# Two small tiles take 64 bytes each, and the output projections' activations start elsewhere in SBUF

## The chip, the cores and the metric

The kernel runs on one core of one Trainium2 chip, as one launch. Its time is device microseconds of one execution; given is the median of a few runs. A separate execution is recorded by the hardware profiler, and all rows below come from that one.

## The reference, cut to what matters

The program is a two-layer decoder trunk over 256 tokens and 1024 channels. Layer 0 mixes tokens by multi-scale retention, layer 1 by a gated delta rule (DeltaNet). A dense SwiGLU channel mixer of 2816 hidden channels follows each. Every sub-layer ends in one large output projection:

```python
    return y.astype(hdn.dtype) @ w_out                      # retention: (256 x 2048) @ (2048 x 1024)
    return o.astype(hdn.dtype) @ w_out                      # DeltaNet:  (256 x 2048) @ (2048 x 1024)
    return (jax.nn.silu(gate) * up) @ w_out                 # SwiGLU:    (256 x 2816) @ (2816 x 1024)
for i in range(DEPTH):                                      # DEPTH = 2
    h = h + mix
    h = h + swiglu(rmsnorm(h, norm_ffn[i]), ffn_w_in[i], ffn_w_out[i])
return rmsnorm(h, norm_final)
```

Everything is float32.

## The kernel before

**Split products.** Each float32 operand of a projection is split into two parts of TensorE's float32r type, hi (rounded) and lo (what is left). A product is then three matmuls (`mm3`, lines 139 to 141): hi by hi, lo by hi, hi by lo. The weights' parts are `whi` and `wlo`, made by ScalarE (line 131) and VectorE (line 133) from a slab `raw` of 512 KB that a DMA brings in. The activations' parts are `xh`/`xl` for the input projections, `yh`/`yl` for the output projection of retention and of DeltaNet, `hh`/`hl` for that of SwiGLU.

**Who is stationary.** In `proj_tok` a block of 128 tokens by 128 channels of the activations is the stationary operand (it is loaded into the array; the trace calls this LDWEIGHTS on PEld), and 512 columns of the weights stream past. So the row `mm<-whi,hh` is a matmul with `whi` moving and `hh` stationary. In `proj_chan` it is the other way round, with 256 columns moving. The four output projections are all made by `out_proj` with `proj_tok`. One slab holds two blocks of 128 channels, and serves 2 blocks x 3 products x 2 halves of the tokens, 12 matmuls. A SwiGLU output projection has 22 channel blocks x 3 x 2 token halves x 2 column halves = 264 matmuls, that of retention or DeltaNet 16 x 3 x 2 x 2 = 192.

**Who waits for whom.** Three buffers each of `raw`, `whi` and `wlo` rotate. TensorE runs its instructions in the order of the program. In the output projections it works through the slabs; transposes and small matmuls of the mixer's last pieces stand between them in the DeltaNet one.

**Where tiles lie.** A tile pool hands out bytes of each partition one tile after another, and each tile's size is rounded up to 32 bytes. The pools of the constants, the weights (`wp`), the input activations (`xp`) and the small scalars (`sm`) live as long as the kernel. Behind them, one pool for each sub-layer (`self.ph`) is opened and closed again. So the end of `sm` is the start of every sub-layer's pool. `rstd` (line 308) allots the tile `ms` (128 x 2 floats) from `sm`, in two buffers; `head` in `retention` allots `brs` (128 x 1 float) from the sub-layer's pool, in two buffers, ahead of `yh` and `yl`.

Of the kernel before, what the change touches and what calls it, by code (L numbers as in the profile page):

```python
# [10 lines left out]
F32 = mybir.dt.float32  # L11
# [6 lines left out]
P = 128  # L18
D = 1024
S = 256  # L20
NT = S // P
# [40 lines left out]
class Trunk:  # L62
# [245 lines left out]
    def rstd(self):  # L308

        nc = self.nc  # L310
        m = self.sm.tile([P, NT], F32, name="ms", tag="ms")
        nc.vector.scalar_tensor_tensor(m, self.ss[:, 0], EPS, self.ss[:, 1], ALU.add, ALU.add)
        r = self.sm.tile([P, NT], F32, name="r", tag="r")
        nc.gpsimd.tensor_tensor(r, m, self.mhalf[:, 0:NT], ALU.pow)
        self.r = r
# [190 lines left out]
    def retention(self, nxt):  # L506
# [4 lines left out]
        tile_ = lambda shape, name, **k: self.ph.tile(shape, F32, name=name, **k)  # L511
# [40 lines left out]
        def head(h, k, q):  # L552
            for _ in range(3):
                yield
            sp = self.psip()
            for j, (c0, i0) in enumerate(((0, 0), (S, P))):
                for d in range(2):
                    nc.tensor.matmul(sp[:, c0:c0 + S - i0], k[:, d, j * P:(j + 1) * P], q[:, d, i0:S],
                                     start=d == 0, stop=d == 1)
            sT = tile_([P, 384], "sT", bufs=2)  # L560
            nc.vector.tensor_tensor(sT[:, 0:S], sp[:, 0:S], b["dec"][:, h], ALU.mult)
            nc.vector.tensor_tensor(sT[:, S:S + P], sp[:, S:S + P], b["dec"][:, h, 0:P], ALU.mult)
            yield
            for t in range(NT):
                op = self.psip()
                nc.tensor.matmul(op, sT[:, t * P:(t + 1) * P], b["v"][0][:, h], start=True, stop=t == 0)
                if t == 1:
                    nc.tensor.matmul(op, sT[:, S:S + P], b["v"][1][:, h], start=False, stop=True)
                st, mv = tile_([P, 6], "bst", bufs=2), tile_([P, 2], "bmv", bufs=2)
                nc.vector.bn_stats(st, op)  # L570
                nc.vector.bn_aggr(mv, st)
                nc.vector.tensor_scalar(mv[:, 1:2], mv[:, 1:2], EPS, None, ALU.add)
                rs = tile_([P, 1], "brs", bufs=2)
                nc.gpsimd.tensor_tensor(rs, mv[:, 1:2], self.mhalf[:, 0:1], ALU.pow)
                yield
                nc.vector.tensor_scalar(b["o"][t][:, h], op, mv[:, 0:1], rs, ALU.subtract, ALU.mult)

        for h in range(4):
            kq = []

            def k_done(ps, kq=kq):
                kq.append(rotate(ps))

            def q_done(ps, kq=kq, h=h):
                self.spawn(head(h, kq[0], rotate(ps)))

            self.proj_chan(w_in, 1024 + h * 256, self.xT, k_done)
            self.proj_chan(w_in, h * 256, self.xT, q_done)
# [633 lines left out]
```

## Time and profile before

| | |
|---|---|
| median of 3 runs | 865.16 us (862.71 to 866.62) |
| the profiled execution, its own time | 866.91 us |
| span of the profile, first to last instruction | 865.2 us |
| TensorE busy | 835.5 us (97%), 4805 matmuls |
| VectorE, ScalarE busy | 567.5 us (66%), 448.8 us (52%) |
| mean granted clock | 0.994 |

The times of the stages, from the span's start: the output projection of retention runs from about 164 to 213 us, that of the first SwiGLU from 337 to 401 us, that of DeltaNet from 624 to 675 us, that of the second SwiGLU from 796 to 858 us. A matmul's row gives its start and a modelled length; matmuls overlap in the array, so the next one starts well before the length is over, and the pace is read from start to start. In a table of windows an instruction counts in a stretch if any of it lies there.

### The profile page before, as it was taken

How to read it: one execution, taken by the hardware profiler on the slowest of the kernel's cores; microseconds unless marked ns; L12 is line 12 of the kernel's file. 1: busy time of each engine (PE TensorE's matmuls, PEld its weight loads, DVE VectorE, ACT ScalarE, POOL GpSimd, SP SyncE). 2: the span in 40 equal slices, each digit the busy share in tenths (PEclk: the TensorE clock that was granted, in tenths of full speed). 3: DMA queues.
4: the chain of work that ended last, by engine and by line, in shares of the span. 5: the costliest groups of instructions: out<-in, count | busy, mean ns of one | idle time of the engine just before them, and what ended most of it. 6: DMA issues, size and time to landing. Idle time of an engine off the chain costs nothing.

```text
span 865.2 us, 12647 instructions
## 1 busy us (share of the span) xinstructions
PE 835.5 (97%) x4805; PEld 709.1 (82%) x4805; DVE 567.5 (66%) x834; ACT 448.8 (52%) x760; POOL 56.9 (7%) x56
## 2 busy tenths in 40 slices
PE   8999999899999999999999989999899999999996
PEld 7789987788788778786999878998788888889885
DVE  4777876575566555555789899864656655666553
ACT  5553234465444443444587755488854644444443
POOL 0000000000000000000117241000110000000000
PEclk9999999999999999999999999999999999999999
DMA  7676456976687778765455734742045687788762
GB/s 257 196 205 172 126 147 171 234 243 179 198 241 230 213 236 230 229 195 148 124 150 140 201 110 117 212 132 90 1 135 182 194 240 228 227 238 245 232 194 74
DMA packets 182367, 158.21 MB, mean 183 GB/s; under 512 B 72690, under 2 KB 126499, under 8 KB 182307
## 3 DMA queue, kind: packets, MB, share of 16 engines
q1 hardware_dynamic: 182130, 157.34, 61.8%
q8 instruction: 37, 0.61, 0.3%
q14 instruction: 24, 0.19, 0.1%
q10 hardware_dynamic: 144, 0.07, 0.0%
q0 software_dynamic: 32, 0.01, 0.0%
HBM read 147.96 MB, written 9.44 MB: 182 GB/s over the span
## 4 chain that ended last, share of the span: by engine, by line
PE 69%; DVE 13%; DMA 8%; ACT 4%; issue 3%; SPq 2%; POOL 1%; POOLq 0%; ACTq 0%; DVEq 0%
PE mm L141 21%; PE mm L140 21%; PE mm L139 21%; DVE wlo L133 5%; DMA ht<-zd 2%; DVE cacc L751 2%; DVE pr L840 2%; SPq L215 2%; ACT whi L131 1%; DMA zd<-z 1%; PE tp L200 1%; DMA raw<-gdn_w_in 1%; DMA raw<-ffn_w_in 1%; DVE Vb L842 1%; PE ip L979 1%
## 5 line engine op out<-in xcount | busy, mean ns | idle before, releaser
L133 DVE TENSOR_TENSOR wlo<-raw,whi 128x1024 fp32r<-128x1024 f32 x260 | 318.0, 1229 | 197.6 <-ACT whi L131 188.6
L131 ACT CAST whi<-raw 128x1024 fp32r<-128x1024 f32 x260 | 271.6, 1050 | 290.8 <-PE mm L140 148.7
L139 PE MATMUL mm<-whi,xh 128*128 128x512 f32 (+1 forms) x576 | 219.1, 383 | 5.0 <-ACT whi L131 4.1
L140 PE MATMUL mm<-whi,xl 128*128 128x512 f32 (+1 forms) x576 | 219.2, 381 | 0.5 <-DVE xl L337 0.3
L141 PE MATMUL mm<-wlo,xh 128*128 128x512 f32 (+1 forms) x576 | 203.4, 381 | 1.8 <-DVE wlo L133 1.7
L139 PEld LDWEIGHTS mm<-whi,xh 128*128 128x128 f32 x576 | 108.9, 189 | 27.1 <-ACT whi L131 6.8
L141 PEld LDWEIGHTS mm<-wlo,xh 128*128 128x128 f32 x576 | 108.6, 189 | 24.9 <-DVE wlo L133 5.1
L140 PEld LDWEIGHTS mm<-whi,xl 128*128 128x128 f32 x576 | 109.0, 189 | 21.6 <-issue 0.7
L139 PE MATMUL mm<-xh,whi 128*128 128x256 f32 x384 | 111.7, 291 | 0.0
L140 PE MATMUL mm<-xh,wlo 128*128 128x256 f32 x384 | 110.1, 287 | 0.3 <-DVE wlo L133 0.2
L141 PE MATMUL mm<-xl,whi 128*128 128x256 f32 x384 | 109.8, 286 | 0.0
L140 PEld LDWEIGHTS mm<-xh,wlo 128*128 128x128 f32 x384 | 74.0, 193 | 2.3 <-issue 1.0
L139 PEld LDWEIGHTS mm<-xh,whi 128*128 128x128 f32 x384 | 74.1, 193 | 1.3 <-issue 0.5
L141 PEld LDWEIGHTS mm<-xl,whi 128*128 128x128 f32 x384 | 74.1, 193 | 0.3
L139 PE MATMUL mm<-whi,hh 128*128 128x512 f32 x176 | 69.6, 396 | 1.0 <-ACT whi L131 1.0
L140 PE MATMUL mm<-whi,hl 128*128 128x512 f32 x176 | 69.5, 395 | 0.0
L141 PE MATMUL mm<-wlo,hh 128*128 128x512 f32 x176 | 63.6, 396 | 0.3 <-DVE wlo L133 0.3
L139 PE MATMUL mm<-whi,yh 128*128 128x512 f32 x128 | 50.0, 398 | 1.0 <-ACT yh L336 1.0
L751 DVE SCALAR_TENSOR_TENSOR cacc<-mm,conv,cacc 128x253 f32<-128x253 f32 (+2 forms) x96 | 45.6, 509 | 8.1 <-ACT cacc L748 7.5
L140 PE MATMUL mm<-whi,yl 128*128 128x512 f32 x128 | 50.6, 395 | 0.0
L141 PE MATMUL mm<-wlo,yh 128*128 128x512 f32 x128 | 48.7, 397 | 0.0
L139 PEld LDWEIGHTS mm<-whi,hh 128*128 128x128 f32 x176 | 33.0, 188 | 9.3 <-ACT whi L131 1.4
(238 smaller groups left out, 857.9 us busy)
## 6 DMA issues: line engine op xcount, KB each, us to landing
raw<-ffn_w_in SPq DMA_DIRECT2D x88, 512.0 KB, 4.4
raw<-ret_w_in SPq DMA_DIRECT2D x48, 512.0 KB, 4.4
raw<-gdn_w_in SPq DMA_DIRECT2D x48, 512.0 KB, 4.0
raw<-ffn_w_out SPq DMA_DIRECT2D x44, 512.0 KB, 4.3
raw<-ret_w_out SPq DMA_DIRECT2D x16, 512.0 KB, 4.3
raw<-gdn_w_out SPq DMA_DIRECT2D x16, 512.0 KB, 3.6
zd<-z SPq DMA_DIRECT2D x52, 128.0 KB, 3.7
ht<-zd SPq DMA_DIRECT2D x13, 512.0 KB, 5.4
```

What stands on the lines that cost most here:

```text
L131: nc.scalar.copy(hi, raw)
L133: lo_ = nc.vector.tensor_tensor(lo, raw, hi.bitcast(F32), ALU.subtract)
L139: t.matmul(out, lh, rh, start=first, stop=False)
L140: t.matmul(out, ll, rh, start=False, stop=False)
L141: self.last_mm = t.matmul(out, lh, rl, start=False, stop=last).ins
L200: self.nc.tensor.transpose(out, in_, self.ident[:n, :n])
L215: nc.sync.dma_start(to[q], z[32 * q:32 * q + 32, 0:nk].rearrange("p k t g i -> p (k t) g i"))
L751: self.nc.vector.scalar_tensor_tensor(acc[:, s:S], ps[:, 0:S - s], cw[:, i, blk:blk + 1], acc[:, s:S], ALU.mult, ALU.add)
L840: V.tensor_tensor(tmp, Vb[:, 0:n, i:i + 1].broadcast_to([P, n, m]), Ab[:, n:32, i].unsqueeze(1).broadcast_to([P, n, m]), ALU.mult)
L842: V.tensor_tensor(Vb[:, 0:n, n:32], Vb[:, 0:n, n:32], tmp, ALU.subtract)
L979: T.matmul(f4(op[:, 2 * j:2 * j + 2]), x(2 * hg + j), f4(st[:, 2 * j:2 * j + 2]), start=True, stop=True)
```

## The change

The tile `ms` is allotted with 16 floats a partition and its first two are used, and the tile `brs` is allotted with 16 floats and its first is used. Two buffers of `ms` so take 128 bytes and not 64, and two of `brs` likewise. Nothing else is edited. On every engine the same instructions stand in the same order with the same waits, so no rows of the order are shown.

```diff
     def rstd(self):
 
         nc = self.nc
-        m = self.sm.tile([P, NT], F32, name="ms", tag="ms")
+
+
+        m = self.sm.tile([P, 16], F32, name="ms", tag="ms")[:, 0:NT]
         nc.vector.scalar_tensor_tensor(m, self.ss[:, 0], EPS, self.ss[:, 1], ALU.add, ALU.add)
...
-                rs = tile_([P, 1], "brs", bufs=2)
+                rs = tile_([P, 16], "brs", bufs=2)[:, 0:1]
                 nc.gpsimd.tensor_tensor(rs, mv[:, 1:2], self.mhalf[:, 0:1], ALU.pow)
```

What moves are start bytes in a partition, read from the two built programs. All tiles of the sub-layers' pools move up by 64, in retention's pool those behind `brs` by 128. Steps between the 128 x 128 blocks of an operand are multiples of 512 bytes, so each block has its tile's remainder.

| tile | start before | mod 128 | mod 256 | start after | mod 128 | mod 256 |
|---|---|---|---|---|---|---|
| `whi`, `wlo` (first buffers) | 44096, 56384 | 64 | 64 | the same | 64 | 64 |
| `xh`, `xl` | 68672, 76864 | 64 | 64 | the same | 64 | 64 |
| `yh`, `yl` of retention | 157248, 173632 | 64 | 64 | 157376, 173760 | 64 | 192 |
| `hh`, `hl`, both SwiGLU layers | 87424, 109952 | 0 | 128 | 87488, 110016 | 64 | 192 |
| `yh` of DeltaNet (first of four) | 157056 | 0 | 128 | 157120 | 64 | 192 |
| `wh`, stationary in DeltaNet's gates, blocks of 128 bytes | 29760 | 64 | 64 and 192 in turn | the same | 64 | 64 and 192 in turn |
| `D`, `A`, `v`, `Vf`, `kT`, `qT`, `Vb` of DeltaNet; `silu`, `z`, `ht` of SwiGLU | | 0 | | | 64 | |
| `cacc`, `vc`, `uu`, `du`, `S1`, `qs`, `pr` of DeltaNet | | 64 | | | 0 | |
| `silu`, `z`, `ht` of retention's end | | 64 | | | 64 | |

## Rows read from the trace of the kernel before

**Rows 1.** The page: busy time by engine; chain that ended last, by engine.
```profile
PE 835.5 (97%) x4805; PEld 709.1 (82%) x4805; DVE 567.5 (66%) x834; ACT 448.8 (52%) x760; POOL 56.9 (7%) x56
...
PE 69%; DVE 13%; DMA 8%; ACT 4%; issue 3%; SPq 2%; POOL 1%; POOLq 0%; ACTq 0%; DVEq 0%
```

**Rows 2.** Groups by line and shape, TensorE: busy us, mean ns | idle before.
```profile
L139 PE MATMUL mm<-whi,xh 128*128 128x512 f32 x512 | 201.0, 396 | 5.0 <-ACT whi L131 4.1 <-ACT xh L655 0.7
...
L139 PE MATMUL mm<-whi,hh 128*128 128x512 f32 x176 | 69.6, 396 | 1.0 <-ACT whi L131 1.0
...
L139 PE MATMUL mm<-whi,yh 128*128 128x512 f32 x128 | 50.0, 398 | 1.0 <-ACT yh L336 1.0
```

**Rows 3.** Windows: length, PE, PEld, DVE, ACT, POOL, granted clock, DMA share, GB/s.
```profile
725.00:775.00 50.00, 50.00 (x222) 41.13 (x221) 28.84 (x26) 23.40 (x25) 0.00 (x0) 1.00 0.81 229
800.00:850.00 50.00, 50.00 (x216) 40.12 (x215) 26.46 (x27) 22.09 (x25) 0.00 (x0) 1.00 0.61 198
350.00:400.00 50.00, 50.00 (x215) 40.03 (x214) 25.88 (x28) 21.73 (x28) 0.00 (x0) 1.00 0.65 206
```

**Rows 4.** Timeline, TensorE, retention's output projection: start us, length us, what.
```profile
174.46 0.40 PE L139 MATMUL mm<-whi,yh 128*128 128x512 f32 x1
...
175.41 0.39 PE L139 MATMUL mm<-whi,yh 128*128 128x512 f32 x1
...
177.02 0.39 PE L140 MATMUL mm<-whi,yl 128*128 128x512 f32 x1
...
179.51 0.39 PE L140 MATMUL mm<-whi,yl 128*128 128x512 f32 x1
```

**Rows 5.** Timeline, TensorE, DeltaNet's output projection.
```profile
667.00 0.39 PE L139 MATMUL mm<-whi,yh 128*128 128x512 f32 x1
...
669.57 0.39 PE L141 MATMUL mm<-wlo,yh 128*128 128x512 f32 x1
```

**Rows 6.** Timeline, TensorE, first SwiGLU's output projection; in brackets idle time before.
```profile
346.97 0.50 PE L139 MATMUL mm<-whi,hh 128*128 128x512 f32 x1 [0.96 <-ACT whi L131]
...
348.42 0.50 PE L141 MATMUL mm<-wlo,hh 128*128 128x512 f32 x1 [0.26 <-DVE wlo L133]
```

**Rows 7.** Chain that ended last, first SwiGLU's output projection: start us, us, what.
```profile
335.59 3.23 DMA zd<-z
338.90 6.01 DMA ht<-zd
...
398.17 0.25 PE mm L141
```

**Rows 8.** Chain that ended last, end of DeltaNet's output projection.
```profile
670.43 0.25 PE mm L141
670.70 0.70 DVE h L360
```

**Rows 9.** Timeline, TensorE, DeltaNet's gates: 32 stationary columns.
```profile
414.90 0.28 PE L139 MATMUL ip<-xh,wh 128*32 128x256 f32 x1
...
415.81 0.28 PE L141 MATMUL ip<-xl,wh 128*32 128x256 f32 x1
```

**Rows 10.** Groups by line and shape, ScalarE.
```profile
L131 ACT CAST whi<-raw 128x1024 fp32r<-128x1024 f32 x260 | 271.6, 1050 | 290.8 <-PE mm L140 148.7 <-PE mm L141 39.1 <-DMA raw<-ffn_w_in 36.8
...
L440 ACT ACTIVATE silu<-mm,r 128x512 f32<-128x512 f32 x20 | 13.7, 685 | 10.3 <-PE mm L141 10.3
...
L617 ACT ACTIVATE silu<-mm,r 128x512 f32<-128x512 f32 x8 | 5.5, 684 | 2.4 <-PE mm L141 2.4
...
L932 ACT COPY D<-tp 128x512 f32<-128x512 f32 x8 | 4.8, 599 | 0.8 <-PE tp L200 0.8
...
L990 ACT COPY S<-ip 128x512 f32<-128x512 f32 x4 | 2.3, 570 | 0.4 <-PE ip L979 0.4
```

**Rows 11.** Groups by line and shape, VectorE.
```profile
L133 DVE TENSOR_TENSOR wlo<-raw,whi 128x1024 fp32r<-128x1024 f32 x260 | 318.0, 1229 | 197.6 <-ACT whi L131 188.6
...
L751 DVE SCALAR_TENSOR_TENSOR cacc<-mm,conv,cacc 128x254 f32<-128x254 f32 x32 | 14.9, 476 | 0.4
```

## The prediction

> **What bounds the kernel now.** I read the page's busy times and its chain first, to know which engine a saving has to be on. TensorE is busy for 835.5 of 865.2 us, and 69% of the chain is its own [rows 1]. Since the change leaves every instruction and every wait where it was, the question is only whether some instruction runs at another pace from another address. So the second view is the groups by shape, TensorE alone. There the stationary operand's name makes no difference to see: 396 ns with `xh`, 396 with `hh`, 398 with `yh` [rows 2]. But these lengths are modelled and overlap (0.39 us long, a start each 0.23 us), so the pace must be counted, not read. Third, therefore, equal windows of 50 us that hold nothing but matmuls of 512 columns: 222 matmuls touch a stretch of the second SwiGLU's input projection (`xh`, `xl` stationary), only 216 and 215 touch stretches of the two SwiGLU output projections (`hh`, `hl` stationary) [rows 3]. TensorE is busy for all of each, at granted clock 1.00, which is the 2.4 GHz level. About 0.39/0.23 = 1.7 matmuls are in flight at any time, so a stretch is touched by that many more than start in it: 50,000/(222 - 1.7) = 227.0 ns, 50,000/(216 - 1.7) = 233.3 ns, and 50,000/(215 - 1.7) = 234.4 ns in the first SwiGLU. I take 233.3 for both and 6.3 ns as the difference, 2.7% of a matmul.
>
> Is it the address, or is it the stage? The two output projections with `yh` tell, since the same code makes them and one lies at 64 modulo 128, the other at 0. In retention (64) two starts that are eleven matmuls apart lie at 177.02 and 179.51: 2.49/11 = 226 ns [rows 4]. In DeltaNet (0) eleven matmuls take from 667.00 to 669.57: 2.57/11 = 234 ns [rows 5]. So the longer pace goes with a stationary operand at 0 in three stages of three, the shorter one with 64 in both. An output projection as such does not have the longer pace. The clock is the same, and the input projection, with the shorter pace, moves more by DMA than the outputs (229 against 198 and 206 GB/s [rows 3]), so DMA traffic isn't the reason either.
>
> **The change part by part.** The padding itself costs nothing: no instruction is added, and the sub-layers' pools still fit. What it moves are start bytes.
>
> *Second SwiGLU's output projection.* 264 matmuls, all on the chain to the end, no wait among them: 264 x 6.3 = 1.66 us.
>
> *First SwiGLU's.* The chain comes into this stage over the last block of hidden channels (a store of `z` at 335.59, the load of `ht` until 344.91) [rows 7], and TensorE stands twice, until 346.97 for `whi` and until 348.42 for `wlo` [rows 6]. What is saved ahead of that is given back in those waits. From there to 398.17, where the chain leaves TensorE [rows 7], I count (398.17 - 348.42)/0.2333 = 213 starts, one of them late: 210 x 6.3 = 1.32 us.
>
> *DeltaNet's.* 192 matmuls. The chain leaves TensorE with the one at 670.43 [rows 8], 15 before the stage's last, so 177 x 6.3 = 1.12 us.
>
> *Restarts.* Retention's stage shows that the shorter pace isn't there at once: from 174.46 to 175.41, shortly after transposes, four matmuls take 238 ns each, and by 177.02 it is 226 [rows 4]. I take six matmuls at the longer pace, 6 ns each, after each break. DeltaNet's stage is broken up by transposes and small matmuls seven times, the SwiGLU ones three times in all: 10 x 6 x 6 ns = 0.36 us that aren't saved. Sum: 1.66 + 1.32 + 1.12 - 0.36 = 3.74 us.
>
> *Retention's output projection.* `yh` and `yl` move by 128 and stay at 64 modulo 128. I take zero; the bounds are 0 and +192 x 6.3 = +1.2 us (second rival).
>
> *VectorE, ScalarE and the DMAs on moved tiles.* The nearest rows for ScalarE are the same activation with `silu` at 0 in SwiGLU (685 ns) and at 64 in retention (684) [rows 10]: no effect. Of PSUM copies the one to `D` (at 0) takes 599 and the one to `S1` (at 64) 570 [rows 10]; since some tiles go from 0 to 64 and as many from 64 to 0, I take zero, with bounds of 29 ns either way. On the 96 taps like the 476 ns row [rows 11], whose `cacc` goes from 64 to 0, and some 70 other instructions of this kind, that is at most 166 x 29 ns = 4.8 us of work either way, mostly beside TensorE. VectorE and ScalarE hold 17% of the whole chain [rows 1], so I keep 4.8 x 0.17 = 0.8 us either way on the path.
>
> *What is late next.* If TensorE needs a slab of 12 matmuls in 12 x 227 = 2.72 us and not 2.80, the cast (1.05 us [rows 10]) and the difference (1.23 us [rows 11]) per slab still fit. The DMA engines are at 0.61 to 0.65 there and run at 0.81 elsewhere without holding TensorE up [rows 3]. So the gain stays, but for DeltaNet's, where TensorE could catch up with the mixer's last pieces; I have no row that gives their slack and leave up to 0.5 us of the 1.12 in doubt.
>
> The profiled execution of 866.91 us (span 865.2, 1.7 around it) would go to 863.2. It lies 1.75 above the median of the runs shown; on that median, 865.16 - 3.74 = 861.4 us, or 0.43% less.
>
> **Rivals.**
>
> *The address isn't the cause: no change, 865.2 us.* For it: the lengths of rows 2 are equal, and the link to the address rests on five stages. Against it: both paces appear in the same code [rows 4, 5]. In the Trainium skill, the page "TensorE: Matmul & The Clock Gate", section "Part 2: What happens when you issue a matmul", gives TensorE two independent SBUF read ports, so that loading the next weights takes nothing from the running matmul, and a gap of 512/2.4 plus about 2.5 ns, some 216 ns, in which no address occurs. By that rule this rival would be the forecast. The trace doesn't agree: it has 227 and 233 ns [rows 3]. The page "SBUF — State Buffer", section "Door 1: The DMA port swizzle", has lines of 16 bytes; 0 and 64 both start a line, so by it too nothing would change.
>
> *It is another modulus: slower.* All operands with the short pace lie at 64 modulo 256, with `whi` and `wlo`, and all with the long one at 128. Afterwards `hh`, `hl` and every `yh`, `yl` lie at 192, which no big matmul of this trace has. If the stationary block must share the weights' place modulo 256, the three stages stay as they are and retention's joins them: 192 x 6.3 = +1.2 us, 866.4 us. It decides the sign as long as the mixer's bound helps by less than 1.2 us; to pass 0.5% (4.3 us) it would need 192 to be worse than 128 by another 912 matmuls' 3.4 ns each. Against it: in DeltaNet's gates the blocks of `wh` lie at 64 and 192 modulo 256 in turn, and eight matmuls over three blocks take 0.91 us, 114 ns each, without a step between blocks [rows 9]. These have 32 stationary columns and not 128, so they weigh little. For 128: 512 moving columns of 4 bytes pass in at most 227 ns, so 64 bytes of them in at most 7.1, and the step between the two paces is 6.3, about one such piece.
>
> *Gained, and given back in DeltaNet's mixer.* The gain of 3.74 is halved by slower taps (+0.8), and by waits for the mixer's last pieces (0.5) and for slabs (0.5): 3.74 - 1.8 = 1.9 us, 863.3 us.
>
> **How the numbers follow.** The forecast has 0.68, no change 0.15, another modulus 0.09, gained and half given back 0.08. The runs shown spread over 3.9 us, so a measured median may be 1 us off; about 0.5% is what a measurement of this kernel can tell from no change, here 4.3 us, a time under 860.8. The forecast's own range, with 0.8 either way for the mixer and 1 for the measurement, is 859.4 to 863.2. To hold eight in ten I go up to 865.7, which takes in more than half of the no-change case, and down to 859.0. Faster by over 0.5%: the forecast lies 0.6 us short of it, about 0.45 of its 0.68 chance, with a little from the rest: 0.33. Slower by over 0.5%: 0.04, nearly all from another modulus. Within: 0.63.
>
> **What would show it.** Right: a 50 us window inside either SwiGLU output projection is touched by 222 matmuls and not 216; eleven matmuls in DeltaNet's output projection take 2.49 us; retention's still do; the waits of the first SwiGLU output projection grow by 0.3 us; everything between 401 and 624 us is as long as before. Wrong: windows still with 216 (no change), or retention's pace at 233 (another modulus), or the right windows with a longer stretch from 401 to 624 us (given back).

## The result, and the profile after

The changed kernel takes 871.29 us (median of 5 runs, 870.13 to 871.83), the kernel before takes 864.72 us (862.35 to 866.62) beside it: ratio 1.0084, 95% interval 1.0062 to 1.0107. It is slower by 6.6 us; 861.4 us was forecast. Its profiled execution took 871.12 us, with a span of 869.4 us, 4.2 more than before. In the profile's page no engine is busy for over 1 us more than before [rows 1], but in the chain that ended last the share of TensorE falls from 69% to 53%, and that of the DMAs rises from 8% to 15%:

```profile
PE 836.4 (96%) x4805; PEld 707.4 (81%) x4805; DVE 567.7 (65%) x834; ACT 448.7 (52%) x760; POOL 57.0 (7%) x56
...
PE 53%; DVE 16%; DMA 15%; ACT 6%; SPq 5%; issue 4%; POOL 1%; POOLq 0%; ACTq 0%; DVEq 0%
```

The windows answer the forecast's first question. These are the input projection of the second SwiGLU and the output projection of the first, with the columns of [rows 3], and then two stretches of DeltaNet's mixer that are spoken of below:

```profile
725.00:775.00 50.00, 50.00 (x222) 41.33 (x221) 30.03 (x28) 23.41 (x25) 0.00 (x0) 1.00 0.82 230
350.00:400.00 50.00, 50.00 (x216) 40.23 (x215) 26.00 (x28) 21.74 (x28) 0.00 (x0) 1.00 0.61 207
...
559.00:562.00 3.00, 3.00 (x71) 2.96 (x64) 2.91 (x8) 1.52 (x2) 0.00 (x0) 0.67 0.71 226
562.00:565.00 3.00, 3.00 (x54) 2.87 (x55) 2.94 (x5) 2.18 (x4) 0.00 (x0) 0.76 0.00 0
```

The output projection is touched by 216 matmuls, as before (215), and not by 222: nothing was gained. Retention's, which had the shorter pace [rows 4], has lost it. In TensorE's timeline of the changed kernel, first retention's output projection, then DeltaNet's, then the place in DeltaNet's mixer:

```profile
177.62 0.39 PE L139 MATMUL mm<-whi,yh 128*128 128x512 f32 x1
...
180.41 0.39 PE L139 MATMUL mm<-whi,yh 128*128 128x512 f32 x1
...
666.34 0.40 PE L139 MATMUL mm<-whi,yh 128*128 128x512 f32 x1
...
669.14 0.40 PE L139 MATMUL mm<-whi,yh 128*128 128x512 f32 x1
...
556.34 0.28 PE L140 MATMUL mm<-xh,wlo 128*128 128x256 f32 x1
558.76 1.20 PE L878 MATMUL ip<-Vc,A 32*32 32x32 f32 x64 [2.14 <-DMA Vc<-Vd]
...
560.40 0.41 PE L140 MATMUL mm<-xh,wlo 128*128 128x256 f32 x1
560.62 0.41 PE L141 MATMUL mm<-xl,whi 128*128 128x256 f32 x1
```

Between the first two rows, and between the next two, lie twelve starts each: 2.79/12 = 232.5 ns in retention (227 before), 2.80/12 = 233.3 ns in DeltaNet (as before). Over all steps of a stage between two big matmuls the means are 232.7, 233.2, 232.6 and 233.2 ns in the four output projections; before they were 227.2, 233.3, 233.3 and 233.3.

The last rows show something that the forecast had no term for. TensorE stands 2.14 us for `Vc`, the solved triangular blocks of DeltaNet, which come back from HBM in another layout. After that the granted clock is 0.67 and 0.76 in the two windows above, so for a part of these 6 us it was at its 1.2 GHz level, and matmuls of 256 columns start each 0.21 to 0.22 us. In the timeline of before the same place has a wait of 0.56 us and a start each 0.12 us:

```profile
557.15 1.20 PE L876 MATMUL ip<-Vc,A 32*32 32x32 f32 x64 [0.56 <-DMA Vc<-Vd]
...
558.62 0.28 PE L140 MATMUL mm<-xh,wlo 128*128 128x256 f32 x1
558.74 0.28 PE L141 MATMUL mm<-xl,whi 128*128 128x256 f32 x1
```

A fall of the clock is nothing that only the changed kernel has, though. Three windows, first of before, then after:

```profile
162.00:167.00 5.00, 4.57 (x13) 3.62 (x14) 4.47 (x7) 4.22 (x8) 0.00 (x0) 0.66 0.87 215
527.00:532.00 5.00, 4.02 (x22) 4.02 (x23) 4.90 (x8) 4.12 (x10) 1.83 (x1) 0.66 0.26 72
557.00:565.00 8.00, 7.26 (x190) 7.01 (x191) 7.81 (x14) 4.95 (x8) 0.00 (x0) 1.00 0.45 128
```

```profile
162.00:167.00 5.00, 4.89 (x21) 3.66 (x22) 4.78 (x7) 4.64 (x8) 0.00 (x0) 1.00 0.73 148
527.00:532.00 5.00, 3.77 (x30) 3.57 (x31) 4.90 (x8) 4.50 (x12) 1.84 (x1) 1.00 0.28 68
557.00:565.00 8.00, 6.24 (x126) 6.10 (x128) 6.20 (x12) 3.70 (x6) 0.00 (x0) 0.79 0.57 138
```

The profile of before has two such falls elsewhere, ahead of retention's output projection and in DeltaNet's mixer, and the profile after has one at `Vc` in place of them. So the clock at `Vc` makes this stretch longer, but in these two profiles it is no part of what the whole kernel lost.

Why `Vc` is late, the chain that ended last says. Before, then after (start, us, what):

```profile
547.85 4.82 DMA Vd<-Vb
552.69 4.33 DMA Vc<-Vd
```

```profile
547.86 5.34 DMA Vd<-Vb
553.22 5.40 DMA Vc<-Vd
```

The pair starts at the same time as before and ends 1.6 us later. `Vc` is written to SBUF in pieces of 128 bytes; so are the stores `zd<-z` of the transposes read from it. The trace records every DMA packet. Those of 128 bytes have a mean duration, before and after, of 12.34 and 13.30 ns in the first SwiGLU's input projection, 12.48 and 13.26 in the second's, 12.12 and 13.33 ns in the store of DeltaNet's `A` (4096 packets at 479 us), and 12.91 and 15.86 ns in the load of `Vc`. These are just the ones whose SBUF side went from 0 to 64 modulo 128. Retention's `z` was at 64 and stayed there: 13.3 and 13.2 ns.

A mean hides how it comes about. With `Vc` at 0 all 4096 packets of its load take 11 to 13 ns; after the change 73% of them still do, and 18% take over 20 ns (27.6 in the mean). And one load doesn't fit: the 1,024 packets of `wr`, the raw weights of DeltaNet's gates, are written in pieces of 128 bytes to a start at 64 modulo 128 (1,024 bytes below `wh`), and take 12.9 to 13.0 ns in all thirteen kernels of this document, also in the two in which `wr` lies at 0. So for a load a start at 64 isn't enough by itself; what else it needs wasn't followed.

Where the spans part, by the first big matmul of each stage, in us (the last column is the best version, below):

| stage | before | after | best |
|---|---|---|---|
| start to retention's output projection | 167.6 | 165.8 | 161.9 |
| retention's output projection | 44.8 | 46.9 | 46.0 |
| first SwiGLU, input | 125.0 | 125.8 | 126.4 |
| first SwiGLU, output, to DeltaNet's first channel projection | 82.7 | 81.6 | 79.2 |
| DeltaNet, the channel projection beside `Vd` and `Vc` | 52.2 | 54.6 | 52.1 |
| DeltaNet, the rest up to its output projection | 151.8 | 151.7 | 151.7 |
| DeltaNet's output projection | 50.4 | 50.3 | 49.3 |
| second SwiGLU, input | 121.7 | 121.8 | 121.6 |
| second SwiGLU, output, to the end | 69.0 | 70.9 | 67.8 |

One execution's stage is good to two or three microseconds: in the eight kernels that leave SwiGLU's `z` at 0, the first SwiGLU's input projection takes 123.3 to 126.8 us.

### The profile page after: what moved, and what is told of

The parts are those of the page before. It is cut to its first block, busy times and chain, and to the rows that moved or that the text cites. A ratio compares the mean times of both kernels' runs of the same rounds, so it can differ in the third digit from the quotient of the medians.

```text
span 869.4 us, 12647 instructions
## 1 busy us (share of the span) xinstructions
PE 836.4 (96%) x4805; PEld 707.4 (81%) x4805; DVE 567.7 (65%) x834; ACT 448.7 (52%) x760; POOL 57.0 (7%) x56
## 4 chain that ended last, share of the span: by engine, by line
PE 53%; DVE 16%; DMA 15%; ACT 6%; SPq 5%; issue 4%; POOL 1%; POOLq 0%; ACTq 0%; DVEq 0%
PE mm L141 15%; PE mm L140 15%; PE mm L139 15%; DVE wlo L133 7%; DMA ht<-zd 5%; SPq L215 4%; DMA raw<-ffn_w_in 4%; DMA zd<-z 3%; ACT whi L131 3%; DVE pr L842 2%; DVE cacc L753 2%; DVE z L210 2%; PE tp L200 1%; DVE Vb L844 1%; PE ip L981 1%
## 5 line engine op out<-in xcount | busy, mean ns | idle before, releaser
L141 PEld LDWEIGHTS mm<-wlo,hh 128*128 128x128 f32 x176 | 33.0, 188 | 9.7 <-DVE wlo L133 1.9
```

Source lines behind the costliest of these rows:

```text
L141: self.last_mm = t.matmul(out, lh, rl, start=False, stop=last).ins
```

## The experiments

Two theories came out of this. **TensorE:** a big matmul has the short pace when the stationary block starts at the same place modulo 256 as the weights that stream past; against it, that 64 modulo 256 (or another fixed place, or a modulus of 512) is what counts. **DMA:** packets of 128 bytes cost more when their SBUF side starts at 64 modulo 128; against it, that the whole loss is TensorE's. Each kernel was timed beside the kernel before. That one's median was 867.99 us beside the four kernels "retention alone", "the hidden activations alone", "all four at 64" and "DeltaNet alone"; 866.70 us beside the repeat, "the weights moved", "the small tiles of SwiGLU alone" and "both theories used, first version"; and 867.28 us beside the two kernels with tiles put back and "both theories used throughout". Paces are means over the steps of a stage.

**The changed kernel again.** No edit.

> The changed kernel once more, beside the others on one chip. If its loss belongs to the addresses, the ratio to the kernel before is again about 1.008 (1.006 to 1.011), with retention's output projection 2 us longer, the stretch of DeltaNet with the store of Vb and the load of Vc 2 us longer and the rest in the SwiGLU layers. If it was the chip or the moment of the first comparison, the ratio is near 1.003, the 2 us of retention's pace alone.

873.89 us, ratio 1.0077 (1.0060 to 1.0093). Paces 232.3 to 232.7 in all four, packets of `z` 13.3 ns, `Vc` lands after 5.33 us. The loss repeats. In this profile it is the two SwiGLU input projections that grew most: 126.6 and 125.0 us, for 125.0 and 121.7 before.

**Retention alone.** `brs` takes 96 bytes, so that retention's `yh`, `yl` lie at 192 modulo 256 and nothing else moves by other than a multiple of 128.

```diff
-                rs = tile_([P, 1], "brs", bufs=2)
+                rs = tile_([P, 24], "brs", bufs=2)[:, 0:1]
```

> Only brs is padded, to 24 floats, so that in retention's pool yh, yl and what lies behind them move by 128: from 64 to 192 modulo 256, the place they have in the changed kernel. Everything else lies as before. Theories A and B: retention's output projection goes from 227 to about 233 ns a matmul, 192 x 6 ns = 1.1 us, up to 2 us with what waits around it, 866 to 867 us. Rival C: no cost, 864.7 us, since nothing changes modulo 128.

868.90 us, ratio 1.0008 (0.9985 to 1.0031). Twelve starts take 2.79 us, 232.5 ns each:

```profile
180.00 0.39 PE L139 MATMUL mm<-whi,yh 128*128 128x512 f32 x1
...
182.79 0.39 PE L139 MATMUL mm<-whi,yh 128*128 128x512 f32 x1
```

So 64 and 192 modulo 256 aren't alike, though both are 64 modulo 128. The stage takes 46.6 us and not 44.8; in the whole time this can't be told from nothing.

**The hidden activations alone, at the weights' place.** 192 bytes ahead of `hh` and 64 behind `hl`, so that these lie at 64 modulo 256 and the tiles behind them keep their remainder.

```diff
+            self.ph.tile([P, 48], F32, name="pad0")
             b["hh"] = self.ph.tile([P, nk, S], F32R, name="hh")
             b["hl"] = self.ph.tile([P, nk, S], F32R, name="hl")
+            self.ph.tile([P, 16], F32, name="pad1")
```

> Only SwiGLU's pool: 192 bytes of padding ahead of hh, hl and 64 behind, so that both lie at 64 modulo 256 and modulo 512, and z, ht, silu keep their place modulo 128. Theories A and B: 227 ns a matmul in both SwiGLU output projections, 264 and 210 matmuls x 6.3 ns = 3.0 us less, 861.7 us. If an operand's place modulo 256 does not set the pace: 864.7 us.

864.68 us, ratio 0.9957 (0.9934 to 0.9979), faster. 227.0 ns in both SwiGLU output projections, 233.4 still in DeltaNet's. This is the gain that the forecast wanted, 1.66 + 1.32 us of it in these two stages, from the address that it takes: 64 modulo 256.

**All four at 64 modulo 256, and the other tiles behind them at 64 modulo 128.** The pools start 64 bytes lower.

```diff
-        m = self.sm.tile([P, NT], F32, name="ms", tag="ms")
+        m = self.sm.tile([P, NT], F32, name="ms", tag="ms", bufs=1)
...
-        r = self.sm.tile([P, NT], F32, name="r", tag="r")
+        r = self.sm.tile([P, NT], F32, name="r", tag="r", bufs=1)
...
-                rs = tile_([P, 1], "brs", bufs=2)
+                rs = tile_([P, 16], "brs", bufs=2)[:, 0:1]
```

> All sub-layers' pools start 64 bytes lower than before (the scalar tiles ms and r have one buffer each), and brs is padded as in the change: hh, hl at 64 modulo 256 (320 modulo 512), DeltaNet's yh, yl likewise, retention's yh, yl at 64 modulo 512 as before; all other tiles of the pools at 64 modulo 128 where they were at 0. Theory A, the pace depends on the stationary block's start modulo 256 (64 short, 0, 128 and 192 long): starts 227 ns apart in all four output projections, about 3.7 us less than before, 861.0 us. Rival B, modulo 512 (only 64 short): long pace of 233 ns in the SwiGLU and DeltaNet output projections, 864.7 us. Rival C, what cost the changed kernel its time is mostly DMAs on tiles that went from 0 to 64 modulo 128 (z, ht, Vb, Vc): 2 to 5 us are added to either, 863 to 866 us under A, 867 to 870 under B.

868.79 us, ratio 1.0021 (0.9996 to 1.0047): no faster, though all four paces are short, 227.1 to 227.2 ns. `hh` lies at 320 modulo 512 here, so 512 isn't the modulus. Packets of `z` take 13.4 ns, and `Vc` lands after 5.51 us. Both theories together would have it at 863 to 866 us on 864.7, a ratio of 0.998 to 1.002. What TensorE gains is lost again, so the loss isn't TensorE's alone.

**The weights moved, the activations of three stages left.** 64 bytes in the pool of the constants put `raw`, `whi`, `wlo`, `xh` and `xl` at 128 modulo 256, and the two `bufs=1` of the last kernel give them back behind, so that the sub-layers' tiles lie as before. (Behind `mhalf` a few constants move by 64 too, `wr`, `wh` and `wl` of the gates among them.)

```diff
         self.mhalf = self.const.tile([P, 16], F32, name="mhalf")
+        self.const.tile([P, 16], F32, name="pad5")
```

> 64 bytes of padding ahead of the weights' buffers, and 64 fewer behind them (ms and r with one buffer): raw, whi, wlo, xh, xl move from 64 to 128 modulo 256, all tiles of the sub-layers' pools stay. Theory A1, the two operands must share their place modulo 256: input projections (128 with 128) and SwiGLU output projections (128 with 128) at 227 ns, retention's output projection (64 with 128) at 233: ratio 0.998. Theory A2, the place 64 modulo 256 itself is the good one: input projections go to 233 ns, some 1700 matmuls x 6.3 ns = 10 us more, SwiGLU's output projections stay at 233: ratio 1.012.

863.97 us, ratio 0.9966 (0.9950 to 0.9982), faster. `hh`, `hl` and DeltaNet's `yh`, `yl` stay where they were, at 128, and their paces fall to 227.1 and 227.3 ns. Forty microseconds of the second SwiGLU's output projection, first of before, then of this kernel:

```profile
805.00:845.00 40.00, 40.00 (x174) 32.05 (x173) 21.85 (x24) 17.49 (x20) 0.00 (x0) 1.00 0.64 210
```

```profile
805.00:845.00 40.00, 40.00 (x178) 33.07 (x177) 22.26 (x23) 17.87 (x21) 0.00 (x0) 1.00 0.67 216
```

Retention's `yh`, still at 64, is off the weights' place now and takes 229.0 ns, longer than 227 but not the 233 that was expected. It is the place relative to the weights that counts, and no fixed one.

**DeltaNet alone.** 64 bytes at the head of its pool.

```diff
+            self.ph.tile([P, 16], F32, name="pad2")
             b["kT"] = self.big("kT", (8, S))
```

> Only DeltaNet's pool moves by 64 bytes, as in the changed kernel: yh, yl from 128 to 192 modulo 256, Vb, Vc, Ab and the like from 0 to 64 modulo 128. Theories A and B: the pace of its output projection stays at 233 ns, no change, 864.7 us. Rival C: the store of Vb and the load of Vc take 10.7 us together and not 9.2, and the stretch up to the output projection is 2.3 us longer, 867 us.

868.51 us, ratio 1.0003 (0.9982 to 1.0024). DeltaNet's `yh` goes to 192 modulo 256 and the pace stays long (232.3 ns). The load and its wait come out much as in the changed kernel (chain, then TensorE's timeline), and the stretch beside them takes 54.2 us for 52.2, the 2 us that were expected; but the whole time shows no loss.

```profile
542.99 5.07 DMA Vd<-Vb
548.07 5.38 DMA Vc<-Vd
```

```profile
553.59 1.20 PE L876 MATMUL ip<-Vc,A 32*32 32x32 f32 x64 [1.85 <-DMA Vc<-Vd]
...
555.93 0.41 PE L139 MATMUL mm<-xh,whi 128*128 128x256 f32 x1
556.15 0.41 PE L140 MATMUL mm<-xh,wlo 128*128 128x256 f32 x1
```

**The small tiles of SwiGLU alone.** 64 bytes behind `hl`: `z`, `ht` and `silu` go to 64 modulo 128, `hh` and `hl` stay.

```diff
             b["hl"] = self.ph.tile([P, nk, S], F32R, name="hl")
+            self.ph.tile([P, 16], F32, name="pad1")
```

> Only SwiGLU's pool, 64 bytes of padding behind hl: z, ht, silu and gb move from 0 to 64 modulo 128, hh and hl stay at 128 modulo 256. Theory C (stores in pieces of 128 bytes are dearer from 64 modulo 128): the 128-byte packets of the SwiGLU layers take 13.3 ns and not 12.4; 45056 packets x 0.9 ns over 16 DMA engines are 2.5 us of each engine's time, of which 1 to 2.5 us reach TensorE as later slabs: ratio 1.001 to 1.003. Without it: 1.000, and a part of the changed kernel's loss stays open.

870.09 us, ratio 1.0039 (1.0021 to 1.0057), slower, and by more than the 0.1 to 0.3% that were expected, with `hh`'s pace unchanged at 233.3 ns. Packets of `z` take 13.4 and 13.3 ns. This edit alone brings about half of the loss, and nothing of it can be TensorE's pace. Nor is it VectorE or ScalarE at the moved tiles: the activation into `silu` takes 685 ns as before, the transpose from `silu` to `z` 1240 for 1238, the difference `hl` from `ht` 1226 for 1225. Of these rows on the moved tiles, the stores' packets are what changed; that the time is lost through them follows from this and was not isolated, since `z`, `ht`, `silu` and `gb` moved together.

**The changed kernel with SwiGLU's small tiles put back.** The same line, added to the changed kernel.

> The changed kernel with 64 bytes more behind hl: z, ht, silu, gb of both SwiGLU layers are back at 0 modulo 128, all else is as changed. Short packets: the stores of z take 12.4 ns a packet again and about half of the loss goes: 1.0035 to 1.005 of before (0.39% less than the changed kernel). Rival (the loss is all TensorE's, retention's output projection and its knock-on): 1.0077 as the changed kernel.

867.49 us, ratio 1.0004 (0.9986 to 1.0022). Packets of `z` are at 12.4 to 12.5 ns again, and the loss is gone, 0.73% less than the repeat, where 0.39% was expected. Retention's pace (232.3 ns) and `Vc`'s landing (5.36 us) are still those of the changed kernel.

**The changed kernel with DeltaNet's tiles put back.** The same line as in the kernel with DeltaNet alone, added to the changed kernel.

> The changed kernel with 64 bytes more at the head of DeltaNet's pool: Vb, Vc and all other tiles of DeltaNet behind it are back at 0 modulo 128 (cacc and its like at 64), its y at 0 modulo 256, still not with the weights. Packets of Vb, Vc: load of Vc back to 4.3 to 4.6 us, the stretch from 401 us to the output projection shorter by 2 us, total 1.005 to 1.006 of before. Rival (the stretch is hidden in the total, as when DeltaNet alone was moved): 1.0077, no change.

871.74 us, ratio 1.0050 (1.0027 to 1.0074). As expected in size, but its interval overlaps that of the changed kernel, so the gain isn't shown. The load is back (chain, and TensorE's wait), the stretch takes 53.1 us:

```profile
546.09 4.75 DMA Vd<-Vb
550.85 4.54 DMA Vc<-Vd
```

```profile
555.52 1.20 PE L878 MATMUL ip<-Vc,A 32*32 32x32 f32 x64 [0.68 <-DMA Vc<-Vd]
...
667.40 0.39 PE L139 MATMUL mm<-whi,yh 128*128 128x512 f32 x1
...
669.92 0.39 PE L141 MATMUL mm<-wlo,yh 128*128 128x512 f32 x1
```

From 667.40 to 669.92 are eleven starts, 229 ns: DeltaNet's `yh` lies at 0 modulo 256 here, 64 below the weights' place.

**Both theories used, first version.** The kernel with the hidden activations at the weights' place, and 64 bytes behind retention's `yl`, so that its `z` and `ht` lie at 0 modulo 128 too.

```diff
                     b["yl"] = self.ph.tile([P, 16, S], F32R, name="yl")
+                    self.ph.tile([P, 16], F32, name="pad4")
```

> SwiGLU's hh, hl at 64 modulo 256 with z, ht at 0 modulo 128 (as in the run that did this alone), and in retention's pool 64 bytes behind yl, so that z, ht, silu go from 64 to 0 modulo 128. Theories A and C together: 3 us less from TensorE's pace, and 12288 packets in retention at 12.4 and not 13.3 ns, 0.7 us of each DMA engine: ratio 0.995 to 0.996, the fastest of all. A alone: 0.9965.

862.16 us, ratio 0.9947 (0.9927 to 0.9967): faster than both kernels. Retention's packets take 12.4 ns, and the 55.8 us ahead of its output projection become 51.3; a part of this is the fall of the clock at 162 us, which the profile of before has and this one hasn't.

**Both theories used throughout.** The kernel with the moved weights, and `brs` of 16 floats: all four output projections share 128 modulo 256 with the weights, and `z` of all sub-layers, `A` and `Vc` lie at 0 modulo 128.

> Weights' parts and input activations at 128 modulo 256 (64 bytes more in the pool of the constants, and one buffer each of ms and r so that the pools behind stay), and brs of retention 16 floats wide: now all four output projections have their stationary operand at 128, as the weights, and z, ht of all sub-layers and Vb, Vc lie at 0 modulo 128. Shared place modulo 256: pace of all four output projections 227 to 227.5 ns; retention's 192 matmuls take 45 us, not longer. Short packets: the stores of z in retention cost 12.4 ns a packet as in the SwiGLU layers. Both theories together: 0.993 to 0.995 of before (three output projections gain up to 3.7 us, retention's stores up to 1 us), some 860 to 862 us. Rival (the TensorE gain is given back by waits for weight slabs, as in the kernel in which all lay at 64): 0.997 to 1.000.

860.55 us, ratio 0.9911 (0.9878 to 0.9943), the best version; 0.993 to 0.995 was expected, which the interval reaches. Paces 227.1, 227.0, 227.3 and 227.0 ns; packets of `z` 12.3 to 12.5 ns in all three sub-layers; TensorE waits 0.58 us for `Vc`. Retention's output projection takes 46.0 us, where 45 was expected. TensorE's busy time falls by 9.8 us. Of these the paces are 4.5 (528 x 6.3 ns in the SwiGLU layers, 192 x 6.0 in DeltaNet); the profile of before also has two falls of the clock, and this one has none until its last matmul. The chain is TensorE's own again:

```profile
PE 825.7 (96%) x4805; PEld 704.5 (82%) x4805; DVE 567.6 (66%) x834; ACT 448.8 (52%) x760; POOL 57.0 (7%) x56
...
PE 70%; DVE 11%; DMA 9%; ACT 5%; issue 3%; SPq 2%; POOL 0%; POOLq 0%; ACTq 0%; DVEq 0%
```

## Why the prediction was wrong

**What bounds the kernel** was right: TensorE, and the pace told by counting starts and not by lengths. That a pace hangs on an address was right too, and the rival by which it doesn't fell: the same matmuls take 227 or 233 ns as the padding wants it.

**"The longer pace goes with a stationary operand at 0 in three stages of three, the shorter one with 64 in both"** is the step that failed. The rows were read rightly, but they fit two rules, and the forecast took modulo 128 on the operand alone. The kernel with the moved weights shows what it was: the same place modulo 256 as the moving weights. All 52 stages of the thirteen kernels (four each) follow it:

| stationary start less the weights', modulo 256 | pace, ns |
|---|---|
| 0 | 226.8 to 227.3 |
| 64 | 233.3 to 233.4 |
| 128 | 232.2 to 233.2 |
| 192 | 229.0 and 229.1 |

**Second SwiGLU 1.66, first SwiGLU 1.32, DeltaNet 1.12:** each was worth next to nothing here. `hh` and DeltaNet's `yh` lay 64 above the weights' place and lie 128 above it, and the pace is long at both (233.3 ns before, 232.6 to 233.2 after). That such a gain is to be had, the kernel with the hidden activations at the weights' place shows (0.43%, 3.7 us, for 2.98 in the terms). The restarts' 0.36 had nothing to be taken from.

**Retention's zero** was wrong, and its upper bound of +1.2 about right: 192 x 5.5 ns = 1.06 us of pace, while the stage grew by 2.1 us and, alone, by 1.8.

**VectorE and ScalarE at zero** held: 567.5 and 567.7 us of VectorE, 448.8 and 448.7 of ScalarE. But the heading of that step named the DMAs on moved tiles, and no number was ever given to them. Here lies the largest part of the loss, as the kernels with SwiGLU's small tiles moved alone and put back show. Two SwiGLU layers store 2 x 22,528 packets of 128 bytes, each about 0.9 ns longer: over 16 engines 2.5 us of every DMA engine's time. In the five kernels with SwiGLU's `z` at 64 the two input projections together take 247.6 to 251.6 us (mean 250.0), in the eight with `z` at 0 they take 245.9 to 248.3 (mean 247.1). The changed kernel's own first profile is the 247.6, only 0.9 more than before: the means and the medians carry this reading, that one profile doesn't. In the Trainium skill, the page "DMA: Bandwidth & Descriptors", section "How a descriptor splits into AXI transactions", lets a transaction begin only at a multiple of 256 bytes, and what lies between that and the start is fetched for nothing. By it, pieces of 128 bytes in a row would need 6 beats of 32 bytes in the mean at 0 modulo 128 and 8 at 64 (an estimate by that rule). For the stores, which read SBUF, the trace agrees in the direction; in size it shows 7% (13.3 ns for 12.4). The section doesn't speak of pieces that are written: there the load of `Vc` shows 23% and that of `wr` nothing.

**The load of `Vc`** already came 0.56 us late for TensorE before. With 1.07 us more on it and 0.52 on `Vd`, the wait grew to 2.14 us, and the granted clock fell behind it: 15 matmuls of 256 columns at 213 ns and not 120, some 1.4 us more in this stretch. In the five kernels with `Vc` at 64 modulo 128 it lands after 5.33 to 5.51 us, in the eight others after 4.3 to 4.6. All five have a wait of 1.8 to 2.4 us there and that fall of the clock right behind it; of the eight others only one has, the kernel with the moved weights, whose `Vd` took 6.57 us in its profile. The other seven wait 0.56 to 1.35 us; in two of them the clock falls 6 to 8 us later, behind further small waits. The channel projection beside it takes 54.2 to 56.0 us in the five, 52.1 to 53.1 in six of the others, and 54.6 and 55.7 in the two whose `Vd` took longest (5.56 and 6.57 us) with `Vc` at 0. That 0.52 us on `Vd` comes from its start isn't shown.

**"What is late next"** looked at weight slabs for a shorter pace that never came. TensorE's wait for `whi` rose from 5.1 us in 4 waits to 6.7 in 9. With SwiGLU's small tiles moved alone it is 5.8 us in 8, and with them put back in the changed kernel 4.6 in 5: the longer stores go with later slabs, as far as one profile each can say.

**The range.** It was to start 1.8 us below 861.4, which is 859.6 and not 859.4; nothing hangs on it.

**The rivals.** "Another modulus" named the very condition, "the stationary block must share the weights' place modulo 256", with what it would do to each stage, and this came; its price of +1.2 us held for TensorE (1.06) and left the DMAs out. Against it stood the gates' blocks at 64 and 192 in turn [rows 9]; blocks of 32 columns with 114 ns a matmul say nothing of 128, and this was too weak a reason to set its chance as low as 0.09.

**What stays open** is the split. Alone, SwiGLU's small tiles cost 0.39%, retention 0.08%, DeltaNet 0.03%, in sum 0.50% with some 0.4% of doubt, and the change costs 0.77 to 0.84%. Undone in the changed kernel, SwiGLU's tiles give back 0.73% and DeltaNet's 0.27%, each with some 0.3% of doubt, so that DeltaNet's can't be told from nothing. By both, SwiGLU's small tiles are the largest part, between 3.4 and 6.3 us; how much the three feed each other isn't settled by these intervals.

## What to carry to other kernels

Before an operand is moved to a remainder "as the others have", list the remainders of both operands of the matmul, modulo 256 as well, and ask which differences the trace of before holds; where two rules fit the same five stages, a kernel that moves the other operand tells them apart. Whatever else is allotted behind a padded tile moves too: price its DMAs by their piece length and start, above all those in pieces of 128 bytes. Padding can serve one tile at a time (in the best version four edited lines, for 0.9%).

## What the runs showed of the hardware

- A float32r matmul of 512 columns, with its 128 x 128 stationary block, starts each 227 ns when both operands start at the same place modulo 256, each 232 to 233 ns at 64 or 128 above, and each 229 ns at 192 above.
- A 128-byte packet read from SBUF by a store of `z` took 12.3 to 12.5 ns in the mean from starts at 0 modulo 128 and 13.2 to 13.4 from 64. One written to SBUF by the load of `Vc` took 12.9 ns in all eight kernels with `Vc` at 0, and 15.2 to 16.2 in the mean in the five with it at 64, where 16 to 21% of the packets took over 20 ns. The load of `wr` took 12.9 to 13.0 ns at either start.
- Work ahead of retention's output projection took 51.2 and 51.3 us in the two kernels with retention's `z` at 0 modulo 128, and 52.5 to 56.3 us in the eleven others. The stores there are 12,288 packets, 0.7 us of each DMA engine's time. In four of the eleven (55.2 to 56.3 us) the clock fell in this stretch; the seven without that fall take 52.5 to 55.3. Why the difference is larger than 0.7 us wasn't followed.
- Behind a wait of 2.14 us on one load the granted clock went to its 1.2 GHz level, and 15 matmuls took 1.4 us longer than at 2.4 GHz. The kernel before lost as much twice elsewhere: (1 - 0.66) x 5 us = 1.7 us of full clock in each of two windows, against (1 - 0.79) x 8 us = 1.7 in the changed kernel's one.
